# The first head's decay made in thirds between the small projections of a hybrid decoder block

## The chip, the cores and the metric

The kernel runs on one core of one Trainium2 chip. Its time is the device time of one execution in microseconds (us); what is compared is the median of three runs. The core has five engines that work beside each other, each through its own instruction queue and in that queue's order: PE (TensorE, matmuls), ACT (ScalarE, functions of single elements), DVE (VectorE, operations on one or two tensors and scans), POOL (GpSimd) and SP (SyncE, which here issues DMA transfers). An engine starts its next instruction when the semaphores that this instruction names have been raised by other engines or by transfers. Matmul results lie in PSUM, all else in SBUF.

## The reference, cut to what matters

A sequence of 1024 tokens with 16 meta tokens ahead of it (1040 columns, `T`) goes through one block: gated linear attention (GLA, 4 heads with 128 key channels and 256 value channels each) beside an mLSTM of 4 heads, then a gated MLP. All is float32. What the change touches is the decay of GLA's first head. `z` is the normalised input:

```python
log_a = jax.nn.log_sigmoid(g_lr @ w_gate + b_gate) / 16     # g_lr: 16 small channels of z @ w_in
bc    = cumsum(log_a)                                       # inside a chunk
score = sum_k q[t,k] * k[s,k] * exp(bc[t,k] - bc[s,k])      # s <= t
out   = (q * exp(bc)) @ S + score @ v
```

The kernel forms the decay as min(y, 0) - ln(1 + exp(-|y|)), which is log sigmoid of y, and sums it with a scan that starts anew at each chunk of 128 tokens.

## The kernel before, in words

**Input and precision.** The normalised input is transposed on PE into `xH` and `xL` (channels on the partitions, 8 tiles of 128 channels, tokens along the free axis): `xH` is the value rounded to PE's faster format, `xL` the rest. A weight is split in the same way, and a product is made of three matmuls (high by high, high by low, low by high).

**Projections.** `proj_cm` (L222) makes one projection in pieces of some 256 tokens. A piece is 24 matmuls (8 channel tiles by 3 products) into one of three PSUM banks (tag `pj`); ACT empties the bank with the bias into `kT` (L545) or `qT` (L554). The first head's key and query projections and the key projection of the second head, `k1`, are interleaved by `together` in `key_query_proj(0)` (L548 on): key, query, key 1, key, query, key 1, and so on. After six of these pieces the small projections stand.

**Small projections.** `small_proj` (L165) makes 40 rows at once: 16 low-rank gate channels and the input and forget gates of the mLSTM. It has three column groups `TH_ALL` of 348, 346 and 346 tokens, each of 16 matmuls into a `pj` bank (tile `plr`); ACT copies the lower half out and DVE adds bias and both halves into `lrs`.

**Decay.** `decay(0)` (L751) multiplies `lrs` by the gate weight: three groups of two matmuls into banks of the tag `s` (tiles `pre`). ACT takes the absolute value of each group, then exp of the whole row, then ln(1 + .) of the whole row, for which it loads another table of functions first; DVE takes the minimum of each group with 0, subtracts, and scans the whole row (`rmask` is 1, and 0 at each chunk's first token) into `bc`. `pack` (L187) copies `lrs` and the gate weight into `raw_s` and `wgp` for the heads that come later; POOL clears both first.

**Masks.** L509 to L531 make six 128x128 masks in the tile `mfs` on POOL, one memset and 22 `affine_select`; DVE copies the first to `flip` and the other five as bytes to `mu16` to `mu1`. `flip` is the matrix by which PE turns a tile of scores around (tile `sct`).

**Token sums.** `token_sums(0, nc.sync)` (L598) is work for a much later stage: eight sums and differences of 514 columns on POOL between the tiles `xa` and `xb`, stored by eight transfers that SP issues (L619). The two tiles have the tag `of` with two buffers. The next tile of that tag is `An` of the first head's scores: it takes the buffer of `xb`, the one after it that of `xa`.

**Scores of head 0.** `gla(0)` (L776) first makes the levels 1 to 64: at each level the product of the decayed key and the decayed query of half blocks of that size, with DVE, POOL and ACT taking parts (`level`, `pk` tiles). Level 1 begins with ACT's exp of the decay into `An` (L856). Then come the diagonal products (`kq`, L789 to L794), the turned tile (`sct`, L819) and PE's column sums of `kq` (L800, tile `sc`).

**What sets the order.** The program is written in generators that yield after each piece, and a scheduler moves instructions on each engine by priority: `hp(n)` lifts what is written inside it by n places, and `tc.issue_after(x)` holds it behind the instruction x. So evacuations and splits move forward, while PE's order stays near the written one. `main` (L1146) runs a projection's pieces and, 1.15 times to a piece, moves the generator at the head of `side`, here `gla(0)`, one step on.

Of the kernel before, what the change touches and what calls it, by code (L numbers as in the profile page):

```python
# [45 lines left out]
def hybrid_kernel(ctx, tc, x, meta, norm_mix, w_in, b_in, gla_w_gate, gla_b_gate, gla_norm,  # L46
# [118 lines left out]
    def small_proj():  # L165
# [5 lines left out]
        for t0, n in TH_ALL:  # L171
            pt = ps.tile([P, 512], F32, name=f"plr{t0}", tag="pj", bufs=3)
            for k in range(NK):
                first, both = (xL, 64), (xH, P)
                for j, (x, m) in enumerate((both, first) if k < NK - 1 else (first, both)):
                    nc.tensor.matmul(pt[:m, :n], lr2[:, k, :m], x[:, k, t0:t0 + n],
                                     start=(k == 0 and j == 0), stop=(k == NK - 1 and j == 1), skip_group_check=True)
            with hp(PRI_E):
                r = lrs[0:64, t0:t0 + n]
                nc.scalar.activation(r, pt[64:128, :n], AF.Copy)  # L180
                nc.vector.scalar_tensor_tensor(r, pt[0:64, :n], bsm[0:64], r, OP.add, OP.add)
            yield
        nc.gpsimd.dma_start(msc, lrs[32:40, :])

    decay_in = {}

    def pack():  # L187

        lrs, K = decay_in[0], NM + 1
        nc.gpsimd.memset(raw_s[0:96].bitcast(F32), 0.0)  # L190
# [316 lines left out]
    with tc.issue_after(last.ins):  # L507

        lmask = {}  # L509
        mfs = hd.tile([P, T], F32, name="mfs", tag="raw", bufs=1)  # L510
# [5 lines left out]
        nc.vector.tensor_copy(flip, mfs[:, :P])  # L516
# [3 lines left out]
        for i, b in enumerate((16, 8, 4, 2, 1)):  # L520
            mf = mfs[:, P * (i + 1):P * (i + 2)]
            nb = P // (2 * b)
            for odd in range(2):
                half = mf[:, 64 * odd:64 * odd + 64].rearrange("p (n w) -> p n w", w=b)
                for base, sg in (((P - 1) * odd, -1), (b - 1 - (P - 1) * odd, 1)):
                    nc.gpsimd.affine_select(out=half, in_=half, compare_op=OP.is_ge, fill=0.0, base=base,
                                            pattern=[[sg * 2 * b, nb], [0, b]],
                                            channel_multiplier=sg if odd else -sg)
            mu = hd.tile([P, P], U8, name=f"mu{b}")
            nc.vector.tensor_copy(mu, mf)  # L530
            lmask[b] = mu  # L531
# [16 lines left out]
    def key_query_proj(s):  # L548
        h = s % 4
        hh = heads.setdefault(s, {})  # L550
        if s < 4:
# [4 lines left out]
            if s == 0:  # L556
                k1 = key_proj(1)
                yield from islice(together(pk, pq, k1), 6)
                yield from small_proj()
                token_sums(0, nc.sync)  # L560
                pkq = together(pk, pq)
                yield from islice(pkq, 1)
                decay(0)
                pack()
                yield from pkq
                side.append(gla(0))
# [183 lines left out]

    def decay(s):  # L751
        la = wtile(f"la{s}")
        pre = []
        for t0, n in TH_ALL:
            pt = ps.tile([P, 512], F32, name=f"pre{s}_{t0}", tag="s", bufs=3)
            if s:
                w, x = wgp[0:65 + NM, P * (s - 1):P * s], raw_s[0:65 + NM]
            else:
                w, x = wg, decay_in[0][0:NM + 1]
# [1342 lines left out]
```

## Time and profile before

| | us |
|---|---|
| median of three runs | 1871.53 |
| lowest and highest run | 1869.77, 1873.11 |
| profiled execution | 1871.91 |
| its span in the trace | 1869.9 |

The granted clock of PE, averaged over the profiled span, is 0.997 of the full one. The rows that the prediction shows are of that execution. Names in them are cut to the program's names: `plr` and `pre` are the PSUM tiles of the small projections and of the decay, `pj` those of the key and query pieces, `la` and `bc` the two rows of the decay, `mfs`, `mu` and `flip` the masks, `xa` and `xb` the token sums, `pk` a level, `pv` the value projection. A row of the timeline gives the start from the beginning of the span, the time of the group, the engine, the tile or operation, and in square brackets the idle time of the engine ahead of it with what ended that.

### The profile page before, as it was taken

What the parts mean: (1) busy time and instruction counts of PE and PEld (TensorE: products, weight loads), DVE (VectorE), ACT (ScalarE), POOL (GpSimd) and SP (SyncE); (2) the same over time, 40 slices, a digit from 0 to 9 for tenths busy, and PEclk for the clock granted to TensorE, in tenths of its full rate; (3) what the DMA queues carried; (4) which work ended last, traced back from release to release, by engine and by line L of the source; (5) the groups of instructions that cost most, each with busy time, mean ns of one, the idle gap of its engine ahead of it and who ended that gap; (6) DMA issues with size and microseconds to landing.
All of it is one profiled execution on the core that took longest, in us unless ns stands there. A gap on an engine that the chain in (4) does not pass through costs nothing.

```text
span 1869.9 us, 32624 instructions
## 1 busy us (share of the span) xinstructions
PE 1847.2 (99%) x13286; PEld 1769.7 (95%) x13286; DVE 1227.2 (66%) x1817; ACT 868.8 (46%) x1394; POOL 429.8 (23%) x485
## 2 busy tenths in 40 slices
PE   8999999999999999999999999999999999999998
PEld 7899999999999999999999999999999999987886
DVE  7756757554563466655432547698887888787876
ACT  5465555545454433432422335543443443465664
POOL 6301101205442000123281510012222222200100
PEclk9999999999999999999999999999999999999999
DMA  5111022143324755665973643324333334288894
GB/s 164 56 37 60 23 61 60 35 116 122 96 77 125 195 139 144 159 181 158 335 240 113 221 152 125 124 86 131 118 103 113 108 102 130 86 321 317 284 385 166
DMA packets 221820, 269.63 MB, mean 144 GB/s; under 512 B 13986, under 2 KB 177101, under 8 KB 221671
## 3 DMA queue, kind: packets, MB, share of 16 engines
q1 hardware_dynamic: 200447, 196.20, 33.9%
q0 software_dynamic: 18624, 62.62, 10.1%
q10 hardware_dynamic: 2600, 8.74, 1.2%
q8 instruction: 104, 1.70, 0.4%
q14 instruction: 45, 0.37, 0.1%
HBM read 197.91 MB, written 69.60 MB: 143 GB/s over the span
## 4 chain that ended last, share of the span: by engine, by line
PE 88%; DVE 5%; DMA 3%; ACT 2%; issue 1%; SPq 0%; POOL 0%; POOLq 0%; ACTq 0%; DVEq 0%
PE pj L232 11%; PE pv L274 8%; PE Yu L1175 6%; PE Xu L1175 6%; PE Zu L1175 6%; PE bg L1414 5%; PE bm L1414 5%; PE Zg L1175 4%; PE Yg L1175 4%; PE Xg L1175 4%; PE po L1708 4%; PE Vu L1175 3%; PE pdX L1865 2%; PE pdZ L1865 2%; PE pdY L1865 2%; PE Vg L1175 2%
## 5 line engine op out<-in xcount | busy, mean ns | idle before, releaser
L638 POOL TENSOR_TENSOR ts<-ts 128x256 f32<-128x256 f32 x88 | 78.6, 899 | 49.4 <-DMA ts<-in_ffn_w_down_dram 47.4
L1621 POOL TENSOR_TENSOR SB<-SA,rg 128x512 f32<-128x512 f32 x20 | 32.7, 1637 | 239.7 <-issue 101.4
L274 PE MATMUL pv<-wH_gv,xH 128*128 128x256 f32 x256 | 75.0, 293 | 0.0
L274 PE MATMUL pv<-wH_mv,xH 128*128 128x256 f32 x256 | 74.8, 292 | 0.1
L880 POOL TENSOR_TENSOR pk<-pk,kT 128x256 f32<-128x256 f32 (+1 forms) x24 | 31.0, 1291 | 187.3 <-ACT pk L878 154.6
L274 PE MATMUL pv<-wH_gv,xL 128*128 128x256 f32 x256 | 72.6, 283 | 0.0
L1708 PE MATMUL po<-wH_wo,yH 128*128 128x256 f32 x256 | 72.5, 283 | 0.1
L274 PE MATMUL pv<-wL_gv,xH 128*128 128x256 f32 x256 | 72.5, 283 | 0.0
L274 PE MATMUL pv<-wL_mv,xH 128*128 128x256 f32 x256 | 71.9, 281 | 0.0
L1708 PE MATMUL po<-wL_wo,yH 128*128 128x256 f32 x256 | 71.7, 281 | 0.3 <-DVE wL_wo L147 0.3
L274 PE MATMUL pv<-wH_mv,xL 128*128 128x256 f32 x256 | 71.9, 281 | 0.0
L1708 PE MATMUL po<-wH_wo,yL 128*128 128x256 f32 x256 | 71.8, 281 | 0.0
L1656 DVE SCALAR_TENSOR_TENSOR cv<-u,fc,cv 128x1024 f32<-128x1024 f32 x44 | 65.1, 1482 | 0.4
L1603 POOL TENSOR_TENSOR A<-u2raw,A 128x512 fp32r<-128x512 f32 x20 | 42.5, 2124 | 86.2 <-ACT A L1602 86.2
L1414 PE MATMUL bg<-ogL,wH_bg 128*128 128x342 f32 x192 | 61.5, 320 | 0.0
L1414 PE MATMUL bg<-ogH,wH_bg 128*128 128x342 f32 x192 | 61.5, 320 | 0.0
L1414 PE MATMUL bm<-omH,wH_bm 128*128 128x342 f32 x192 | 61.4, 320 | 0.0
L1414 PE MATMUL bm<-omH,wL_bm 128*128 128x342 f32 x192 | 61.3, 319 | 0.0
L1414 PE MATMUL bg<-ogH,wL_bg 128*128 128x342 f32 x192 | 61.3, 319 | 0.0
L1414 PE MATMUL bm<-omL,wH_bm 128*128 128x342 f32 x192 | 61.2, 319 | 0.0
L278 DVE TENSOR_TENSOR v<-pv,bB 128x256 f32<-128x256 f32 x64 | 26.5, 417 | 40.3 <-PE pv L274 40.0
L1602 ACT ACTIVATE HA<-rg 128x1024 fp32r<-128x1024 f32 x16 | 17.0, 1061 | 73.0 <-PE Yu L1175 72.6
(814 smaller groups left out, 7511.5 us busy)
## 6 DMA issues: line engine op xcount, KB each, us to landing
gw<-in_w_in_dram SPq DMA_DIRECT2D x26, 512.0 KB, 5.4
ts<-in_ffn_w_down_dram POOLq DMA_DIRECT2D x44, 256.0 KB, 3.9
tdn<-ts POOLq DMA_DIRECT2D x44, 256.0 KB, 3.1
rg<-in_ffn_w_up_dram SPq DMA_DIRECT2D x22, 512.0 KB, 3.9
ru<-in_ffn_w_up_dram SPq DMA_DIRECT2D x22, 512.0 KB, 3.9
adr<-s SPq DMA_DIRECT2D x40, 256.0 KB, 3.0
rd<-in_ffn_w_down_dram SPq DMA_DIRECT2D x20, 512.0 KB, 11.4
do<-tdn SPq DMA_DIRECT2D x18, 512.0 KB, 5.5
```

Of the source, the lines that this page charges most:

```text
L232: nc.tensor.matmul(pt[:, :n], a[:, k, :], b[:, k, base + t0:base + t0 + n], start=(i == 0), stop=(i == 3 * NK - 1))
L274: nc.tensor.matmul(pt[:, :DV], a[:, k, t0:t0 + P], b[:, k % 4, :], start=(i == 0), stop=(i == 3 * NK - 1))
L278: nc.vector.tensor_tensor(vt[:n, c, :DV], pt[:n, :DV], bB[:n, :], OP.add)
L638: nc.gpsimd.tensor_tensor(t[:, o], t[:, a], t[:, b], OP.subtract)
L880: eng.tensor_tensor(e, e, k, OP.mult)
L1175: nc.tensor.matmul(out[:, :n], x[:, k, :], y[:, k, :], start=start and k == 0 and j == 0, stop=stop and k == 3 and j == 2, skip_group_chec ...
L1414: nc.tensor.matmul(pt[:, i, :n], a[:, k, :], b[k][:, base + t0:base + t0 + n], start=(k == 0 and j == 0), stop=(k == NK - 1 and j == 2))
L1603: eng.tensor_tensor(l, src, h.bitcast(F32), OP.subtract)
L1621: late.tensor_tensor(sb[:, 0:4], sa[:, 0:4], rg[:, 0:4], OP.subtract)
L1656: nc.vector.scalar_tensor_tensor(y, u[:, j:SEQ + j], fc[:, j, jj:jj + 1], y, OP.mult, OP.add)
L1708: nc.tensor.matmul(pt[:, :DV], a, b[:, k % 4, :], start=(k == 0 and i == 0), stop=(k == NK - 1 and i == len(terms) - 1))
L1865: nc.tensor.matmul(banks[r, j, b][:, c], p, q[:, c], start=first and k == 0, stop=last and k == 2, skip_group_check=True)
```

## The change

The first head's decay gets a function of its own, `first_decay`. It is a generator with one step for each third of the columns: a `pre` product, ACT's Abs and Exp and DVE's minimum of that third. It is advanced once after the second and once after the third small projection, so that the first two thirds are made there; the last third follows after one key piece, where the whole decay stood. The logarithm, the subtraction and the scan are then made in two halves (columns 0 to 528 and 528 to 1040; at 528 a chunk begins, so the second scan starts at 0).

The small projections come after five pieces of the interleaved projections in place of six; the sixth (second piece of `k1`) follows the first head's last key and query pieces. `raw_s` is cleared by a function of its own, `clear`, which is called ahead of the small projections. The tile `mfs` takes a buffer of the tag `r`, which an input tile had, in place of `raw`. The copies of the masks on DVE (`keep_masks`) are held behind the last sum of the small projections (`joined`), the token sums behind the clearing and the last `affine_select` (`masked`). `decay`, for the other heads, is the same but for the branch that head 0 had.

```diff
--- before.py
+++ after.py
@@ -178,16 +178,18 @@
             with hp(PRI_E):
                 r = lrs[0:64, t0:t0 + n]
                 nc.scalar.activation(r, pt[64:128, :n], AF.Copy)
-                nc.vector.scalar_tensor_tensor(r, pt[0:64, :n], bsm[0:64], r, OP.add, OP.add)
+                joined[:] = [nc.vector.scalar_tensor_tensor(r, pt[0:64, :n], bsm[0:64], r, OP.add, OP.add).ins]
             yield
         nc.gpsimd.dma_start(msc, lrs[32:40, :])
 
-    decay_in = {}
+    decay_in, joined = {}, []
+
+    def clear():
+        return nc.gpsimd.memset(raw_s[0:96].bitcast(F32), 0.0)
 
     def pack():
 
         lrs, K = decay_in[0], NM + 1
-        nc.gpsimd.memset(raw_s[0:96].bitcast(F32), 0.0)
         nc.gpsimd.memset(wgp.bitcast(F32), 0.0)
         src = lrs[64:64 + K, :3 * P]
         for p0 in (0, 32):
@@ -507,13 +509,12 @@
     with tc.issue_after(last.ins):
 
         lmask = {}
-        mfs = hd.tile([P, T], F32, name="mfs", tag="raw", bufs=1)
+        mfs = hd.tile([P, T], F32, name="mfs", tag="r", bufs=2)
         nc.gpsimd.memset(mfs[:, :P * 6], 1.0)
         for sg in (1, -1):
             nc.gpsimd.affine_select(out=mfs[:, :P], in_=mfs[:, :P], compare_op=OP.is_ge, fill=0.0, base=-sg * (P - 1),
                                     pattern=[[sg, P]], channel_multiplier=sg)
         flip = hd.tile([P, P], F32, name="flip")
-        nc.vector.tensor_copy(flip, mfs[:, :P])
         mu = hd.tile([P, P], U8, name="mu0")
         nc.vector.tensor_copy(mu, ident)
         lmask[0] = mu
@@ -523,12 +524,15 @@
             for odd in range(2):
                 half = mf[:, 64 * odd:64 * odd + 64].rearrange("p (n w) -> p n w", w=b)
                 for base, sg in (((P - 1) * odd, -1), (b - 1 - (P - 1) * odd, 1)):
-                    nc.gpsimd.affine_select(out=half, in_=half, compare_op=OP.is_ge, fill=0.0, base=base,
+                    masked = nc.gpsimd.affine_select(out=half, in_=half, compare_op=OP.is_ge, fill=0.0, base=base,
                                             pattern=[[sg * 2 * b, nb], [0, b]],
                                             channel_multiplier=sg if odd else -sg)
-            mu = hd.tile([P, P], U8, name=f"mu{b}")
-            nc.vector.tensor_copy(mu, mf)
-            lmask[b] = mu
+            lmask[b] = hd.tile([P, P], U8, name=f"mu{b}")
+
+    def keep_masks():
+        nc.vector.tensor_copy(flip, mfs[:, :P])
+        for i, b in enumerate((16, 8, 4, 2, 1)):
+            nc.vector.tensor_copy(lmask[b], mfs[:, P * (i + 1):P * (i + 2)])
 
 
     osc = {g: dram.tile([NK, P, NP], F32, name=f"osc{g}") for g in "gm"}
@@ -555,14 +559,25 @@
                 qT[:, t0:t0 + n], p, AF.Identity, bias=cc(C_GQ + h), scale=QS))
             if s == 0:
                 k1 = key_proj(1)
-                yield from islice(together(pk, pq, k1), 6)
-                yield from small_proj()
-                token_sums(0, nc.sync)
+                yield from islice(together(pk, pq, k1), 5)
+                parts = first_decay()
+                with tc.issue_after(last.ins):
+                    cleared = clear()
+                for i, _ in enumerate(small_proj()):
+                    if i:
+                        next(parts)
+                    yield
+                with tc.issue_after(joined[0]):
+                    keep_masks()
+                with tc.issue_after(cleared.ins), tc.issue_after(masked.ins):
+                    token_sums(0, nc.sync)
                 pkq = together(pk, pq)
                 yield from islice(pkq, 1)
-                decay(0)
+                for _ in parts:
+                    pass
                 pack()
                 yield from pkq
+                yield from islice(k1, 1)
                 side.append(gla(0))
                 yield from k1
             else:
@@ -748,15 +763,33 @@
     def state(name):
         return hd.tile([P, DV + 1], F32, name=name, tag="S", bufs=4)
 
+    def first_decay():
+
+        la = wtile("la0")
+        bc = hd.tile([P, T], F32, name="bc0", tag="bc")
+        heads.setdefault(0, {})["decay"] = la, bc
+        for t0, n in TH_ALL:
+            pt = ps.tile([P, 512], F32, name=f"pre0_{t0}", tag="s", bufs=3)
+            nc.tensor.matmul(pt[:, :n], wg, decay_in[0][0:NM + 1][:, t0:t0 + n], start=True, stop=True)
+            with hp(PRI_E):
+                l = la[:, t0:t0 + n]
+                nc.scalar.activation(l, pt[:, :n], AF.Abs)
+                exped = nc.scalar.activation(l, l, AF.Exp, scale=-1.0)
+                lowest = nc.vector.tensor_scalar(bc[:, t0:t0 + n], pt[:, :n], 0.0, None, OP.min)
+            yield
+        half = NM + SEQ // 2
+        with hp(PRI_E), tc.issue_after(exped.ins), tc.issue_after(lowest.ins):
+            for c in (slice(0, half), slice(half, T)):
+                nc.scalar.activation(la[:, c], la[:, c], AF.Ln, bias=one1)
+                nc.vector.tensor_tensor(la[:, c], bc[:, c], la[:, c], OP.subtract)
+                nc.vector.tensor_tensor_scan(bc[:, c], rmask[:, c], la[:, c], 0.0, OP.mult, OP.add)
+
     def decay(s):
         la = wtile(f"la{s}")
         pre = []
         for t0, n in TH_ALL:
             pt = ps.tile([P, 512], F32, name=f"pre{s}_{t0}", tag="s", bufs=3)
-            if s:
-                w, x = wgp[0:65 + NM, P * (s - 1):P * s], raw_s[0:65 + NM]
-            else:
-                w, x = wg, decay_in[0][0:NM + 1]
+            w, x = wgp[0:65 + NM, P * (s - 1):P * s], raw_s[0:65 + NM]
             nc.tensor.matmul(pt[:, :n], w, x[:, t0:t0 + n], start=True, stop=True)
             pre.append((pt, t0, n))
         if s == 3:
```

The order on three engines, around the copies and around An. First POOL, from the masks to the end of the token sums (`xa`, `xb`); before:

```order
L604 TENSOR_TENSOR xa_682<-xH,xL 128x514
L412 TENSOR_TENSOR xr_365<-xv_363,mhalf 128x1
L511 MEMSET mfs 128x768
L513 AFFINE_SELECT mfs<-mfs 128x128
L526 AFFINE_SELECT mfs<-mfs 128x64 x2
L513 AFFINE_SELECT mfs<-mfs 128x128
L526 AFFINE_SELECT mfs<-mfs 128x64 x18
L604 TENSOR_TENSOR xa_682<-xH,xL 128x514
L607 TENSOR_TENSOR xb_683<-xa_682 128x514
L604 TENSOR_TENSOR xb_683<-xH,xL 128x514
L604 TENSOR_TENSOR xa_682<-xH,xL 128x514
L607 TENSOR_TENSOR xa_682<-xb_683,xa_682 128x514
```

and with the change:

```order
L513 MEMSET mfs 128x768
L188 MEMSET raw_s 96x1040
L515 AFFINE_SELECT mfs<-mfs 128x128
L527 AFFINE_SELECT mfs<-mfs 128x64 x2
L515 AFFINE_SELECT mfs<-mfs 128x128
L527 AFFINE_SELECT mfs<-mfs 128x64 x18
L619 TENSOR_TENSOR xa_669<-xH,xL 128x514 x2
L622 TENSOR_TENSOR xb_670<-xa_669 128x514
L619 TENSOR_TENSOR xb_670<-xH,xL 128x514
L619 TENSOR_TENSOR xa_669<-xH,xL 128x514
L622 TENSOR_TENSOR xa_669<-xb_670,xa_669 128x514
L622 TENSOR_TENSOR xb_670<-xb_670 128x514
```

The first sum of `xa` has moved behind the masks, and the clearing of `raw_s`, which stood before the last two sums, into the masks.

Second DVE, from the masks' copies to the decay; before:

```order
L516 COPY flip<-mfs 128x128
L530 CAST mu_402<-mfs 128x128
...
L530 CAST mu_426<-mfs 128x128
L181 SCALAR_TENSOR_TENSOR lrs<-plr_624,bsm,lrs 64x348
L181 SCALAR_TENSOR_TENSOR lrs<-plr_643,bsm,lrs 64x346
L181 SCALAR_TENSOR_TENSOR lrs<-plr_662,bsm,lrs 64x346
L198 TENSOR_TENSOR raw_s<-lrs,raw_s 17x1040
L769 TENSOR_SCALAR bc_733<-pre_0_727 128x348
```

and with the change:

```order
L181 SCALAR_TENSOR_TENSOR lrs<-plr_638,bsm,lrs 64x346
L533 COPY flip<-mfs 128x128
L778 TENSOR_SCALAR bc_632<-pre_348_657 128x346
L535 CAST mu_401<-mfs 128x128
...
L535 CAST mu_421<-mfs 128x128
L200 TENSOR_TENSOR raw_s<-lrs,raw_s 17x1040
L778 TENSOR_SCALAR bc_632<-pre_694_713 128x346
L784 TENSOR_TENSOR la_631<-bc_632,la_631 128x528
L784 TENSOR_TENSOR la_631<-bc_632,la_631 128x512
L785 SCALAR_TENSOR_TENSOR bc_632<-rmask,la_631 128x528
```

The copy to `flip` and the five casts have moved from ahead of the sums of the small projections to between the second and the last third of the decay; the row L785 is the first half of the scan.

Third ACT, from the last third of the decay to An; before:

```order
L768 ACTIVATE la_726<-pre_694_731 128x346
L770 ACTIVATE la_726<-la_726 128x1040
L771 ACT_TABLE_LOAD
L771 ACTIVATE la_726<-la_726,one_79 128x1040
L554 ACTIVATE qT_441<-pj_514_752,col 128x256
L856 ACT_TABLE_LOAD
L856 ACTIVATE An_856<-la_726 128x512
```

and with the change:

```order
L776 ACTIVATE la_631<-pre_694_713 128x346
L777 ACTIVATE la_631<-la_631 128x346
L783 ACT_TABLE_LOAD
L783 ACTIVATE la_631<-la_631,one_79 128x528
L783 ACTIVATE la_631<-la_631,one_79 128x512
L889 ACT_TABLE_LOAD
L889 ACTIVATE An_861<-la_631 128x512
L558 ACTIVATE qT_435<-pj_514_731,col 128x256
```

The evacuation of the query piece from 514 on, which frees a `pj` bank, stood ahead of the second table load and now stands behind An.

## The prediction, made before the changed kernel was run

> **What bounds the kernel now.** I read the busy table first.
>
> ```profile
> span 1869.9 us, 32624 instructions
> PE 1847.2 (99%) x13286; PEld 1769.7 (95%) x13286; DVE 1227.2 (66%) x1817; ACT 868.8 (46%) x1394; POOL 429.8 (23%) x485
> ```
>
> The matrix engine (PE) is busy for 99% of the span and the change takes no matmul away, so all it can win is PE's idle time, or PE time at a lowered clock. The profiled execution took 1871.91 us: 2.0 more than its span, 0.4 more than the median of the runs, 1871.53. Next the windows (start and end, length, busy time of PE, weight loads, DVE, ACT and POOL, then the granted clock, DMA share, GB/s), cut in steps of 3.41 us, on whose edges the clock changes:
>
> ```profile
> 30.47:33.88 3.41, 1.98 (x18) 1.96 (x18) 3.00 (x7) 3.07 (x7) 0.62 (x2) 1.00 0.29 75
> ...
> 88.50:91.91 3.41, 1.67 (x4) 0.53 (x4) 2.60 (x6) 0.63 (x1) 1.30 (x1) 1.00 0.00 0
> 91.91:95.33 3.42, 2.74 (x9) 2.14 (x10) 3.34 (x5) 2.17 (x3) 0.00 (x0) 0.50 0.00 0
> 95.33:98.74 3.41, 3.41 (x17) 3.31 (x16) 1.73 (x3) 1.46 (x5) 0.00 (x0) 0.50 0.00 0
> ```
>
> One place behind the change stands out: PE is half idle from 88.5 us on, and then runs at half clock from 91.91 to 98.74. The timeline of PE (start, time taken, instruction, and in brackets how long PE was idle and for whom) shows the scores of head 0 there, waiting for the vector engine (DVE):
>
> ```profile
> 87.36 0.28 PE L274 MATMUL pv<-wH_gv,xL 128*128 128x256 f32 x1
> 89.68 1.12 PE L819 MATMUL sct<-A,flip 128*128 128x512 f32 x2 [2.04 <-DVE A L846]
> 91.14 0.50 PE L800 MATMUL sc<-kq,ones 128*128 128x512 f32 x1 [0.34 <-ACT kq L793]
> 91.87 0.79 PE L800 MATMUL sc<-kq,ones 128*128 128x512 f32 x1 [0.22 <-DVE kq L794]
> 93.34 0.80 PE L800 MATMUL sc<-kq,ones 128*128 128x512 f32 x1 [0.68 <-ACT kq L793]
> ```
>
> Now the chain that ended last, for the price of PE's pieces at full clock:
>
> ```profile
> 40.51 7.57 PE plr L176 x48
> 48.08 2.80 PE pj L232 x24
> 50.88 1.94 PE pre L760 x6
> 52.83 8.72 PE pj L232 x72
> ...
> 100.26 0.89 PE sc L829 x8
> 101.15 2.84 PE pv L274 x24
> ```
>
> The product that starts at 87.36 gives way after 2.84/24 = 0.12, at 87.48. From there to 98.7 PE does the two sct matmuls (1.1), four column sums of 512 columns (0.9 by the pv step, which has 256), eight score matmuls (0.9) and some twelve value products (1.4): 4.3 us of work in 11.1 (to 98.6). So **6.8 us are lost here**, half in waits and half in clock. That is the most that this change can win.
>
> DVE is late because it has no slack: from 65.5 on it works at the levels of head 0, 23.5 of 24.1 us.
>
> ```profile
> 65.50:89.60 24.10, 22.08 (x185) 21.58 (x183) 23.50 (x42) 8.92 (x11) 9.99 (x6) 1.00 0.23 64
> ```
>
> These levels begin when the decay is scanned, on DVE, and its logarithm made, on the scalar engine (ACT):
>
> ```profile
> 57.56 1.24 DVE L772 TENSOR_TENSOR la<-bc,la 128x1040 f32<-128x1040 f32 x1 [2.91 <-ACT la L771]
> 58.84 2.32 DVE L773 TENSOR_TENSOR_SCAN bc<-rmask,la 128x1040 f32<-128x1040 f32 x1
> ```
>
> ```profile
> 56.37 1.17 ACT L771 ACTIVATE la<-la,one 128x1040 f32<-128x1040 f32 x1
> 57.44 0.45 ACT L554 ACTIVATE qT<-pj,col 128x256 f32<-128x256 f32 x1
> 58.87 1.28 ACT L856 ACT_TABLE_LOAD   x1 [0.98 <-issue]
> 60.17 0.67 ACT L856 ACTIVATE An<-la 128x512 f32<-128x512 f32 x1
> 61.20 0.22 ACT L921 ACTIVATE dl<-bc 128x8 f32<-128x8 f32 x1 [0.36 <-DVE bc L773]
> ```
>
> ACT's dl at 61.20 starts as the scan ends (61.16), and the weights and levels stand behind it. Call d the shift of that moment. The second kq, which PE takes at 93.34, moves by d too.
>
> **The change, part by part.**
>
> *The projections one piece ahead.* A key piece of 24 matmuls (2.80) now stands behind the small projections, which start about 3.1 earlier, at 37.4 (two small transposes are 0.3 of it). PE's work stays the same. The last `pre` would end at 52.83 - 3.1 = 49.7, and the three pieces behind it (8.72 in the row, 2.81 each) at 58.2.
>
> *The decay by parts.* The first two thirds of Abs and Exp run on ACT between the small projections; there PE feeds ACT, which has room. Behind the last third stand on ACT 0.4 (Abs), 0.4 (Exp), 1.28 (table), and the logarithm in halves of 0.6: 50.0 to 53.3. On DVE two subtractions (0.64 each) end at 54.0 and two half scans (1.17 each) at 56.3, against 61.16. The three further ACT and two further DVE instructions are inside these times. With nothing else in the way d would be -4.8.
>
> *The copies and POOL.* This is where the gain can be lost. The masks' tile moves to a buffer that an x tile leaves just as early, so the masks start as before, but now `raw_s` is cleared ahead of them, and all eight token sums come behind them; one of the eight used to run earlier, in a gap.
>
> ```profile
> 34.01 0.74 POOL L511 MEMSET mfs<- 128x768 f32 x1
> ...
> 42.87 1.30 POOL L604 TENSOR_TENSOR xa<-xH,xL 128x514 f32<-128x514 f32 x1
> ...
> 49.24 0.96 POOL L190 MEMSET raw_s<- 96x1040 f32 x1
> 50.16 1.28 POOL L607 TENSOR_TENSOR xb<-xb 128x514 f32<-128x514 f32 x1
> 51.52 2.20 POOL L607 TENSOR_TENSOR xa<-xa,xb 128x514 f32<-128x514 f32 x1
> ```
>
> 34.75 + 0.95 + 8.1 of selects = 43.7; five sums took 6.37, so 1.27 each, and eight end at 53.9 if nothing stops them. Meanwhile DVE wants to copy the masks:
>
> ```profile
> 42.93 1.33 DVE L530 CAST mu<-mfs 128x128 uint8<-128x128 f32 x1 [1.77 <-POOL mfs L526]
> ...
> 51.34 1.23 DVE L198 TENSOR_TENSOR raw_s<-lrs,raw_s 17x1040 fp32r<-17x1040 f32 x1 [2.16 <-ACT raw_s L197]
> ```
>
> The cast that met a sum took 1.33, as long as the sum, and the sum that met DVE's `raw_s` took 2.20 instead of 1.28: one engine stops while the other runs. Much later sums and DVE's short `wt` steps met as well:
>
> ```profile
> 548.28 2.76 DVE L1038 SCALAR_TENSOR_TENSOR wt<-MB,tcol,big 128x128 f32<-128x128 f32 x2
> ```
>
> Two steps of 128 columns took 2.76 in all, one sum's length for each: they take turns. Of the Trainium skill, the page "SBUF — State Buffer", section "Who interferes with whom", states this as a lock: DVE with two SBUF inputs, or copying in a two-port mode, and POOL exclude each other for a whole instruction, in order of issue. That speaks against this change, and by it alone the half scans would be held up as well, about 1.3 us for each turn lost; the rows above show casts and subtractions held, no scan.
>
> I take turns as the likeliest. The flip copy and five casts are asked for from 47 us on (behind the third small projection), in the middle of the sums. Each cast waits for one sum: they end at about 54.2, `raw_s` (1.1) at 55.3, the last minimum (0.5) at 55.8, the two subtractions at 57.0, the scans at 59.3. In exchange the sums are stopped little and end at 54. Then ACT: table 57.0 to 58.3, An to 59.0, and qT, which now stands behind An on ACT, to 59.4. So d = 59.4 - 61.2 = **-1.8**.
>
> *PE's new wait.* Key 1's next piece, at 58.2, needs the bank that this qT empties: it waits until 59.5, **1.3**. Later, unhindered, PE would reach the second kq at 87.48 + 1.1 + 0.45 = 89.05, now at 90.35; kq is there at 93.3 - 1.8 = 91.5: **1.15** more. The clock stays full, I assume: a window with PE busy 1.98 of 3.41 (30.47) was followed by full clock, one with 1.67 (88.50) by half. The Trainium skill's page "TensorE: Matmul & The Clock Gate", section "HAM oscillation", asks only that no idle gap exceed about 3.4 us. By it these two gaps cost no clock either, but the 2.04 before sct did, so here the row decides.
>
> *Sum.* Lost after: 1.3 + 1.15 = 2.45; lost before: 6.8. 1871.91 - 4.35 = 1867.6 in the profiled execution's terms, less the 0.4: **1867.2**. Behind the scores nothing is added.
>
> Bounds. If POOL and DVE never met, the last store that An's buffer waits for (the seventh sum, 52.6, and the store) would set An:
>
> ```profile
> tsc<-xb SPq DMA_DIRECT2D x2, 128.0 KB, 1.9
> ```
>
> Two issues 0.4 apart and 1.9 of landing: 55.0; table, An and qT to 57.4, no new wait of PE, d = -3.8, kq at 89.5: 0.45 lost, 1865.2. If DVE kept the port from the casts through the scans, see the first rival.
>
> **Rivals.**
>
> *An waits for the store (the slower side).* An's buffer was xb: its stores must land first. If DVE's casts and `raw_s` run in one go, sums six and seven start after 50.5 us; if the subtractions and scans (to 56.5) then shut POOL out as well, the seventh sum ends at 57.8, its store lands near 60.2, and ACT stands still, with qT behind the wait: table to 61.5, An to 62.2, qT to 62.7. PE idles from 58.2 to 62.7, 4.5; a window almost without work is followed by half clock until a full one has passed (as 91.91 to 98.74), some 5.4 us of work at half rate, 2.7. With another sum's delay (1.3) it is 8.5 lost against 6.8: 1873.2. It decides when the store lands later than 60. For it, a POOL product of 1.2 that DVE's row of subtractions and products held up:
>
> ```profile
> 76.74 3.11 POOL L880 TENSOR_TENSOR pk<-pk,kT 128x256 f32<-128x256 f32 x1 [3.98 <-ACT pk L878]
> ```
>
> Against it: the turns above.
>
> *No conflict:* 1865.2, as above. For it: no row shows a scan held up, and the sums' own needs in the row at 42.87 were met in full.
>
> *The gain is used up on the way* (the change does not do what it says): casts, `raw_s` and scans are pushed so far that the scan ends near 61 again, d = 0: 4.25 lost at kq in any case, and half clock for one window (1.7) more: 1870.7. For it: all of these stand in one row on DVE, before the subtractions.
>
> **How the numbers follow.** Forecast 0.43 (1866 to 1868.6), store 0.22, no conflict 0.18, used up 0.17. The range goes from 1864.7 (no conflict, less the spread) to 1873.2, the slower rival; the forecast's own is 1866.0 to 1868.6. About 0.2% (3.7 us) is what a measurement here tells from no change: faster means below 1867.8, slower above 1875.3. Faster: no conflict 0.18 and two thirds of the forecast, 0.29, together 0.47. Slower: 0.11, the tail of the store rival with a second half-clock stretch. The rest, 0.42, is the same.
>
> **What would show it.** Right: An starts near 58.3 and the scans end near 59.3; casts of about 1.3 each between the sums; a wait of PE of 1 to 2 us on ACT's qT near 58; at sct no wait for A, one of about 1 for kq; no half clock. Wrong: An after 61 with ACT waiting for a DMA (first rival); casts of 0.3 and scans done by 57 (no conflict); sct still waiting for DVE's A by over a microsecond (used up). A loss anywhere behind 105 us would be none of these.

## The result, and the profile of the changed kernel

The changed kernel took 1866.42 us (median of 7 runs, 1863.82 to 1868.84) against 1871.53 before (also 7 runs): a ratio of 0.997, with a 95% interval from 0.9958 to 0.9981. It is faster by some 5 us, 0.3%; the prediction was 1867.2. The profiled execution took 1867.16, 4.75 less than that of before. Its busy table shows the same work in a shorter span:

```profile
span 1865.1 us, 32629 instructions
PE 1846.0 (99%) x13286; PEld 1768.5 (95%) x13286; DVE 1227.9 (66%) x1819; ACT 869.8 (47%) x1397; POOL 427.5 (23%) x485
```

The place that the prediction had marked is closed. PE's timeline at head 0's scores, in the changed kernel, answers to the four waits shown of before (2.04, 0.34, 0.22 and 0.68):

```profile
86.55 1.02 PE L852 MATMUL sct<-A,flip 128*128 128x512 f32 x2
87.01 1.03 PE L833 MATMUL sc<-kq,ones 128*128 128x512 f32 x2
88.26 0.50 PE L833 MATMUL sc<-kq,ones 128*128 128x512 f32 x1 [0.21 <-ACT kq L826]
```

One wait of 0.21 is left, and the windows (PE busy first, granted clock third from the end) show full clock where half was granted from 91.91 to 98.74:

```profile
88.50:91.91 3.41, 3.41 (x27) 3.17 (x27) 3.02 (x6) 2.35 (x6) 0.00 (x0) 1.00 0.00 0
91.91:95.33 3.42, 3.42 (x31) 3.42 (x30) 2.16 (x3) 1.83 (x3) 0.00 (x0) 1.00 0.00 0
```

What lies ahead of it, first on DVE from the copy to `flip` on:

```profile
45.83 1.29 DVE L533 COPY flip<-mfs 128x128 f32<-128x128 f32 x1
47.05 0.50 DVE L778 TENSOR_SCALAR bc<-pre 128x346 f32<-128x346 f32 x1
47.48 3.65 DVE L535 CAST mu<-mfs 128x128 uint8<-128x128 f32 x5
51.16 2.22 DVE L200 TENSOR_TENSOR raw_s<-lrs,raw_s 17x1040 fp32r<-17x1040 f32 x1
53.41 0.52 DVE L778 TENSOR_SCALAR bc<-pre 128x346 f32<-128x346 f32 x1
53.84 1.30 DVE L784 TENSOR_TENSOR la<-bc,la 128x528 f32<-128x528 f32 x2
55.06 2.37 DVE L785 TENSOR_TENSOR_SCAN bc<-rmask,la 128x528 f32<-128x528 f32 x2
```

Then two of POOL's token sums beside them, and ACT at the same place:

```profile
49.61 1.30 POOL L622 TENSOR_TENSOR xb<-xb 128x514 f32<-128x514 f32 x1
50.99 1.29 POOL L622 TENSOR_TENSOR xa<-xa,xb 128x514 f32<-128x514 f32 x1
```

```profile
55.21 1.28 ACT L889 ACT_TABLE_LOAD   x1 [2.13 <-DVE la L784]
56.51 0.68 ACT L889 ACTIVATE An<-la 128x512 f32<-128x512 f32 x1
57.09 0.46 ACT L558 ACTIVATE qT<-pj,col 128x256 f32<-128x256 f32 x1
```

The copies and `raw_s` are slowed (3.65 for five casts, 2.22 for a product that took 1.23 before), the sums are not, and the scan ends at 57.43 instead of 61.16. The table load before An waits for DVE's subtraction, not for a store. Nothing waits for `qT`, but it is close: `qT` is done at 57.55, and the next piece starts in its bank at 57.92.

Behind the scores PE was 7.3 us ahead of the execution before, and 7.1 still near 1640; the span shrank by 4.8. The difference was lost in one place there, where the up projection hands over to the down projection. ACT there waits for a transfer, PE for ACT, and then PE runs at half clock for one window; the rows of ACT, of PE and of the windows (cut on the edges of that fall) in the changed kernel, and PE's row of before:

```profile
1639.94 1.06 ACT L1877 ACTIVATE dw<-dy 128x1024 fp32r<-128x1024 f32 x1 [2.88 <-DMA dy<-adr]
```

```profile
1641.05 0.51 PE L1898 MATMUL pdV<-dy,dw 128*128 128x512 f32 x1 [1.74 <-ACT dw L1877]
```

```profile
1639.32:1642.73 3.41, 1.16 (x4) 0.68 (x5) 1.70 (x3) 2.51 (x3) 0.00 (x0) 1.00 1.04 402
1642.73:1646.14 3.41, 3.41 (x10) 2.63 (x9) 3.41 (x4) 3.41 (x4) 0.00 (x0) 0.50 1.04 416
```

```profile
1647.07 0.50 PE L1865 MATMUL pdV<-dy,dw 128*128 128x512 f32 x1 [0.68 <-ACT dw L1844]
```

From the start of the up projection's last matmul to that of the 23rd of the down projection, which is called the handover below, PE took 6.99 us before and 9.60 here. Of these 2.6 some 1.7 are the 3.41 at half clock (an estimate: half of that window), the rest is the longer wait. No step of the prediction knew of this loss; whether it belongs to the change is one of the questions below.

### The profile page after: what moved, and what is told of

Same layout as the page of the kernel before. It is cut to its first block, busy times and chain, and to the rows that moved or that the text cites. A ratio compares the mean times of both kernels' runs of the same rounds, so it can differ in the third digit from the quotient of the medians.

```text
span 1865.1 us, 32629 instructions
## 1 busy us (share of the span) xinstructions
PE 1846.0 (99%) x13286; PEld 1768.5 (95%) x13286; DVE 1227.9 (66%) x1819; ACT 869.8 (47%) x1397; POOL 427.5 (23%) x485
## 5 line engine op out<-in xcount | busy, mean ns | idle before, releaser
L1447 PE MATMUL bm<-omL,wH_bm 128*128 128x342 f32 x192 | 61.2, 319 | 0.0
```

The source lines that it names most:

```text
L1447: nc.tensor.matmul(pt[:, i, :n], a[:, k, :], b[k][:, base + t0:base + t0 + n], start=(k == 0 and j == 0), stop=(k == NK - 1 and j == 2))
```

## The experiments

Each kernel is the changed one with the edit shown. Medians are of 6 to 12 runs; the kernel before took 1871.7 to 1871.8 beside E1 to E8, 1871.05 beside E9 and E10. To compare the executions free of what happens at the start and at the end, three numbers are read from each trace. The **start** is the matmul from which PE has the same 360 matmuls left up to the transposes of `kh` (tile `k0t`), behind head 0's scores: 52.75 before, 52.24 with the change. The **lag** is the end of the scan less this start. The **stretch** is PE's time from the start to `k0t`:

```profile
103.83 0.27 PE L932 MATMUL k0t<-ident,kh 128*16 128x128 f32 x1
```

```profile
96.52 0.27 PE L965 MATMUL k0t<-ident,kh 128*16 128x128 f32 x1
```

So it took 51.1 before (103.83 - 52.75) and 44.3 with the change (96.52 - 52.24); the least in any run is 44.2.

| kernel | scan ends | lag | stretch above 44.2 | handover | median |
|---|---|---|---|---|---|
| before | 61.2 | 8.4 | 6.9 | 7.0 | 1871.5 |
| changed | 57.4 | 5.2 | 0.1 | 9.6 | 1866.4 |
| E1 whole logarithm and scan | 57.5 | 5.4 | 0.4 | 5.9 | 1865.2 |
| E2 piece put back | 58.8 | 6.8 | 2.9 | 5.9 | 1868.6 |
| E3 copies ahead | 60.1 | 3.9 | 0.0 | 7.6 | 1870.1 |
| E4 sums as memsets | 55.9 | 3.9 | 0.0 | 8.9 | 1865.8 |
| E5 sums later | 59.4 | 7.1 | 9.9 | 7.6 | 1875.5 |
| E6 minimum six times | 61.9 | 8.0 | 3.9 | 6.6 | 1868.6 |
| E7 first sum ahead | 57.1 | 4.2 | 0.0 | 7.2 | 1866.8 |
| E8 no thirds | 58.9 | 6.9 | 1.8 | 6.2 | 1866.4 |
| E9 changed, again | 57.7 | 5.2 | 0.0 | 7.8 | 1866.0 |
| E10 before, again | 63.1 | 8.5 | 6.8 | 7.2 | 1870.4 |

### E1: the halves undone

```diff
-            for c in (slice(0, half), slice(half, T)):
+            for c in (slice(0, T),):
```

> The changed kernel with logarithm, subtraction and scan of the first head made whole again, everything else as changed. Theory (what counts is when the scan ends, and ahead of it DVE is busy with the product for raw_s and the last minimum until 53.9 us anyway): the whole logarithm ends near 52.9, the subtraction runs 53.9 to 55.1, the scan ends near 57.4 as in the changed kernel; time within 0.5 us of the changed kernel's 1866.4. Rival (the halves carry the gain, since subtraction and logarithm overlap): the scan ends 1.2 later, at 58.6, PE waits about 1 us more at head 0's scores, near 1867.6.

Measured: 1865.16, ratio 0.9969 (0.9958 to 0.998). DVE's rows of this run:

```profile
53.86 1.24 DVE L784 TENSOR_TENSOR la<-bc,la 128x1040 f32<-128x1040 f32 x1
55.13 2.32 DVE L785 TENSOR_TENSOR_SCAN bc<-rmask,la 128x1040 f32<-128x1040 f32 x1
```

The scan ends where it does with halves (57.45). DVE is busy with `raw_s` and the last minimum until 53.9, and by then the whole logarithm is done. The median lies 1.3 below the changed kernel's, outside the 0.5 expected, but the two intervals against the kernel before nearly coincide. The halves bring 0.3 of the stretch at most, and nothing that the medians show.

### E2: the key piece put back

```diff
-                yield from islice(together(pk, pq, k1), 5)
+                yield from islice(together(pk, pq, k1), 6)
...
-                yield from islice(k1, 1)
```

> The changed kernel with six pieces ahead of the small projections again, so that the decay starts one key piece (2.8 us) later. Theory (part of the 2.8 is given back because the copies then meet fewer token sums): scan ends near 58.8 against 57.4, PE waits 1 to 1.5 us for kq at the scores, no half clock: 1867.0 to 1868. Rival (the piece ahead is nearly the whole gain): scan ends at 60.2, PE waits 2.5 to 3 us and the clock falls to half again: 1869.5 or more.

Measured: 1868.55, ratio 0.9984 (0.9975 to 0.9993). The scan ends at 58.80, as the theory said, but PE's waits at the scores come to 2.2, more than it said:

```profile
87.22 1.12 PE L851 MATMUL sct<-A,flip 128*128 128x512 f32 x2 [0.63 <-DVE A L878]
88.69 0.50 PE L832 MATMUL sc<-kq,ones 128*128 128x512 f32 x1 [0.35 <-ACT kq L825]
89.42 0.50 PE L832 MATMUL sc<-kq,ones 128*128 128x512 f32 x1 [0.23 <-DVE kq L826]
90.89 0.50 PE L832 MATMUL sc<-kq,ones 128*128 128x512 f32 x1 [0.98 <-ACT kq L825]
```

All four waits of before are there. The first is much smaller (0.63 for 2.04), the middle two are the same, the last is larger (0.98 for 0.68), and the clock stays full. The piece ahead is worth some 2.8 of the stretch, although it moves the scan by only 1.4: with the piece back, the copies meet fewer sums and `raw_s` takes 1.23.

### E3: the copies of the masks ahead of the sums again

```diff
         flip = hd.tile([P, P], F32, name="flip")
+        nc.vector.tensor_copy(flip, mfs[:, :P])
...
             lmask[b] = hd.tile([P, P], U8, name=f"mu{b}")
+            nc.vector.tensor_copy(lmask[b], mf)
...
-                with tc.issue_after(joined[0]):
-                    keep_masks()
```

> The changed kernel with the copies of the masks ahead of the sums of the small projections again. Theory: DVE stands before the casts until the last select of POOL (41.9 us), so the first sum of the small projections, at 39.34 in the changed kernel, is made at 42.1 and PE waits about 1.4 us for it ahead of the first product of the decay; behind that DVE meets fewer token sums and the scan still ends near 57. Time 1.2 to 1.5 us above the changed kernel: 1867.6 to 1868. Rival (PE has other work there): no wait of PE above 0.3 at 41 us, the scan ends earlier than 57.4, time within 0.4 of the changed kernel.

Measured: 1870.05, ratio 0.9991 (0.9983 to 1.0), 3.6 above the changed kernel. DVE's last cast waits for POOL's last select, then meets a sum; PE waits for what stands behind it, and the window after runs at half clock:

```profile
41.87 1.29 DVE L532 CAST mu<-mfs 128x128 uint8<-128x128 f32 x1 [1.75 <-POOL mfs L528]
43.08 1.05 DVE L181 SCALAR_TENSOR_TENSOR lrs<-plr,bsm,lrs 64x348 f32<-64x348 f32 x2
```

```profile
43.70 1.03 PE L771 MATMUL pre<-lrs,wg 17*128 17x348 f32 x2 [2.55 <-DVE lrs L181]
```

```profile
44.10:47.50 3.40, 3.40 (x12) 2.52 (x11) 0.55 (x2) 0.95 (x2) 3.32 (x4) 0.52 0.22 77
```

The place of the wait was as expected, its price not: 2.55 and the clock in place of 1.4; the start moves from 52.2 to 56.2. Behind it nothing is lost, for the lag is only 3.9. With the small projections one piece earlier, the copies have to stand behind their sums: without that edit most of the gain is gone. (What it would do alone, without the piece ahead, no run shows.)

### E4: POOL without reading

```diff
-            nc.gpsimd.tensor_tensor(dst, x, y, OP.subtract)
+            nc.gpsimd.memset(dst, 0.5) if k == 0 else nc.gpsimd.tensor_tensor(dst, x, y, OP.subtract)
```

and the same for the additions.

> The changed kernel with the eight token sums of the first channel tile on POOL replaced by memsets of the same tiles (these sums are left out of the computation), so that POOL reads nothing there. Theory (POOL's sums hold DVE up, and after the change the scores have no loss left to win): casts take about 0.2 each, raw_s 1.1 instead of 2.22, the scan ends near 56.2, 1.2 earlier, and the time stays within 0.5 us of the changed kernel's 1866.4. Rival (the decay still sets PE's end): the time falls by about 1.0 to 1865.4. If memsets hold DVE up like sums, casts of 1.3 remain.

Measured: 1865.82, ratio 0.9968 (0.9957 to 0.998). DVE's rows:

```profile
46.32 0.76 DVE L535 CAST mu<-mfs 128x128 uint8<-128x128 f32 x5
47.37 1.23 DVE L200 TENSOR_TENSOR raw_s<-lrs,raw_s 17x1040 fp32r<-17x1040 f32 x1 [0.30 <-ACT raw_s L199]
...
53.49 2.37 DVE L786 TENSOR_TENSOR_SCAN bc<-rmask,la 128x528 f32<-128x528 f32 x2
```

Five casts take 0.76 instead of 3.65, `raw_s` 1.23 instead of 2.22; the scan ends at 55.86, 1.6 earlier, held by the logarithm alone. Of the 1.6 some 0.2 are this execution's earlier start; the lag is 1.3 shorter. The median is 0.6 lower, between the two expectations and within the scatter of the runs. The trace decides: the stretch was 0.1 above its floor and is now on it. (The memsets were done before the casts began, so this run shows what the casts cost without POOL, not what memsets do to them; E5 shows that.) So the meetings of DVE and POOL cost the decay 1.3 us and the kernel 0.1 at most.

### E5: the store rival made on purpose

```diff
         first, second = T0, T0 + 512
+        if k == 0:
+            for _ in range(12):
+                nc.gpsimd.memset(a[1], 0.5)
```

> The changed kernel with twelve memsets of 0.5 us on POOL put among the first token sums, so that the last six sums and the stores that An's buffer waits for come some 6 us later; nothing is left out. This is the first rival of the prediction made on purpose: sums beside the raw_s product, the subtractions and the scans. By the prediction's price: the store lands behind 60, An starts at 61.5 or later, PE stands 3 to 5 us for the query piece's bank at 58 and loses another 1 to 3 at half clock: the time rises by 5 to 8 us over the changed kernel's 1866.4, to 1871.5 or more. The rival reading (PE has enough other work and An is not waited for): An late, but PE waits less than 1 us and the time stays within 1 us. Apart from that it shows whether sums hold up subtractions (0.7 becomes 1.3 or more) and scans (1.2 becomes 2 or more), which no trace so far shows.

Measured: 1875.45, ratio 1.0019 (1.001 to 1.0028), 9 above the changed kernel and one more than the 5 to 8 expected. ACT, PE, and DVE beside POOL:

```profile
62.90 1.28 ACT L892 ACT_TABLE_LOAD   x1 [9.78 <-DMA tsc<-xb]
```

```profile
65.27 0.58 PE L234 MATMUL pj<-xH,wH_gk 128*128 128x256 f32 x1 [7.15 <-ACT qT L558]
```

```profile
52.54 2.42 DVE L787 TENSOR_TENSOR la<-bc,la 128x528 f32<-128x528 f32 x2 [2.06 <-ACT la L786]
54.87 4.51 DVE L788 TENSOR_TENSOR_SCAN bc<-rmask,la 128x528 f32<-128x528 f32 x2
```

```profile
56.06 2.25 POOL L619 TENSOR_TENSOR xa<-xH,xL 128x514 f32<-128x514 f32 x1
```

The slower rival of the prediction is a real mechanism: An waits for the store of `xb`, `qT` stands behind An, and PE behind `qT`'s bank for 7.15 us, with the clock at half when it goes on (0.50 from 65.00 to 68.41). Scans and subtractions are held by sums, and sums by them (two half scans in 4.51 instead of 2.37, a sum in 2.25 instead of 1.29). The changed kernel escapes because its seventh sum ends at 50.91, before the subtractions begin at 53.84. How much room that leaves can be estimated from the rows. In E5 the table load started 2.45 after the end of the sum (60.45); 2.45 after 50.91 is 53.36, and the changed kernel's load started at 55.21, so that An has 1.9 to spare. `qT` has another 0.4. If nothing else moves, some 2.2 us more of POOL work ahead of that sum would make PE wait for the bank; the memsets of E5 came to 6.9.

### E6: aimed at the forecast's own state

```diff
-                lowest = nc.vector.tensor_scalar(bc[:, t0:t0 + n], pt[:, :n], 0.0, None, OP.min)
+                for _ in range(6 if t0 > 348 else 1):
+                    lowest = nc.vector.tensor_scalar(bc[:, t0:t0 + n], pt[:, :n], 0.0, None, OP.min)
```

> The changed kernel with the last minimum made six times over on DVE (the same values), so that the scan ends some 2.2 us later, near 59.6: the state that the prediction had forecast (59.3). By the prediction's price PE then waits about 1.3 for the query piece's bank and 1.15 at the scores: behind the scores PE stands some 2.2 later than in the changed kernel, near 1868.6. The theory now, from the run with the piece put back (scan end 58.8, four waits of 2.2 in all at the scores): 1.3 to 1.8 at the bank and 2 to 3 at the scores, 3.5 to 4.5 later, near 1870.

Measured: 1868.62, ratio 0.9986 (0.9977 to 0.9995). The median is the prediction's price, 2.2 above the changed kernel, yet by another way. The order on ACT changed with the edit, and `qT` came ahead of An again:

```profile
54.62 0.46 ACT L558 ACTIVATE qT<-pj,col 128x256 f32<-128x256 f32 x1
59.65 1.28 ACT L890 ACT_TABLE_LOAD   x1 [4.57 <-DVE la L785]
```

So PE never waited for the bank of `qT`. It waited 0.42 for that of a key piece (at 62.98) and lost the rest of the 3.9 at the scores, where two waits of 0.23 and 0.97 were followed by a window of half clock:

```profile
89.42:92.83 3.41, 2.17 (x7) 0.88 (x6) 2.88 (x5) 1.82 (x4) 0.00 (x0) 1.00 0.00 0
92.83:96.24 3.41, 3.41 (x16) 3.31 (x16) 1.81 (x3) 1.35 (x3) 0.00 (x0) 0.50 0.00 0
```

This execution had started 1.6 later from its first loads on, and its lag of 8.0 is above the 6.8 that the forecast amounts to. It neither bears out nor refutes the wait of 1.3 at the bank.

### E7: the first token sum ahead again

```diff
-                with tc.issue_after(cleared.ins), tc.issue_after(masked.ins):
-                    token_sums(0, nc.sync)
+                token_sums(0, nc.sync)
```

> The changed kernel with the token sums no longer held behind the masks and the clearing, so that the first of them runs at 29 to 31 us again as in the kernel before. Theory: PE's gaps for the normalised x tiles at 30 to 34 us return (about 1.3 us, the start of the small projections moves from 35.9 to about 37), and the sums end 1.3 earlier; the scan ends within 0.5 of 57.4, PE arrives later at the scores by about 0.7 and waits no more there: time within 1 us above the changed kernel. Rival (holding the sums back matters only for the copies): no gap at 30 us, time the same or 0.5 lower because casts meet fewer sums.

Measured: 1866.84, ratio 0.9975 (0.9966 to 0.9984). PE's gap for an x tile is back, as it was in the kernel before, while the sums end earlier and leave `raw_s` alone:

```profile
31.27 0.63 PE L425 MATMUL xtp<-ident,xt 128*128 128x128 f32 x4 [1.43 <-DVE xt L417]
```

```profile
51.78 1.23 DVE L200 TENSOR_TENSOR raw_s<-lrs,raw_s 17x1040 fp32r<-17x1040 f32 x1
```

In the changed kernel this gap is 0.42. Of that 1.0 some 0.6 is left at the start (52.86 against 52.24), and the lag of 4.2 is worth nothing. By the medians the two are not told apart.

### E8: the thirds in one row

```diff
-                for i, _ in enumerate(small_proj()):
-                    if i:
-                        next(parts)
-                    yield
+                yield from small_proj()
```

> The changed kernel with all three thirds of the first head's decay made where the last one stands, behind the key piece; pieces, copies, sums and halves as changed. Theory: three Abs and three Exp then stand on ACT ahead of the table load and three minima on DVE behind the raw_s product; subtractions start near 54.9 to 55.3 instead of 53.8, the scan ends near 58.7, and PE loses some 2 us more at the scores (as with the piece put back): 1868 to 1869. Rival (the thirds change nothing, since DVE is held until 53.4 in any case): scan end within 0.4 of 57.4, time within 0.5 of the changed kernel.

Measured: 1866.43, ratio 0.9973 (0.9964 to 0.9982). The scan ends at 58.86, as the theory said:

```profile
46.38 5.18 DVE L535 CAST mu<-mfs 128x128 uint8<-128x128 f32 x5
53.99 1.37 DVE L775 TENSOR_SCALAR bc<-pre 128x348 f32<-128x348 f32 x3
56.50 2.36 DVE L782 TENSOR_TENSOR_SCAN bc<-rmask,la 128x528 f32<-128x528 f32 x2
```

The stretch is 1.7 longer than the changed kernel's. The start is 0.3 earlier, because PE does the six small products in one place. That leaves 1.4 in the trace, and none in the median. By the trace the thirds are worth something, by the time it isn't shown.

Two things in this run bear on the prediction. Its lag, 6.9, is that of E2 and of the forecast, yet PE waits only twice at the scores, not for A, and the clock stays full:

```profile
88.17 0.50 PE L830 MATMUL sc<-kq,ones 128*128 128x512 f32 x1 [0.23 <-DVE kq L824]
89.64 0.51 PE L830 MATMUL sc<-kq,ones 128*128 128x512 f32 x1 [0.97 <-ACT kq L823]
```

And its casts took 5.18, not 3.65: three in a row waited for one sum each.

### E9 and E10: both kernels again, unaltered

> The changed kernel once more, unaltered. Theory: all that the change does lies before 92 us and repeats within 0.3 (scan end 57.4, no wait of PE above 0.3 at the scores); the 2.5 us that the first profile of the changed kernel lost near 1640, where ACT waits for a transfer, belong to that execution: the time from the last Zu product to the tenth row of the down projection lies anywhere between 5.9 and 9.6, as in the runs so far. Rival (arriving earlier makes PE wait there): it is 9 or more again.

> The kernel before once more, unaltered. Theory: the loss of 6 to 7 us at head 0's scores with a stretch of half clock is there again (scan end 8.4 behind PE's piece, within 0.3), and the stretch near 1645 differs by chance. Rival: the half clock was a matter of that one execution, and the loss is 4 us or less now.

Measured: 1866.02, ratio 0.9978 (0.9968 to 0.9988), and 1870.42, ratio 1.0 (0.9991 to 1.0009). PE's rows at the scores, first of the changed kernel, then of the one before:

```profile
88.50 0.50 PE L833 MATMUL sc<-kq,ones 128*128 128x512 f32 x1 [0.18 <-ACT kq L826]
```

```profile
91.62 1.13 PE L819 MATMUL sct<-A,flip 128*128 128x512 f32 x2 [2.02 <-DVE A L846]
93.08 0.50 PE L800 MATMUL sc<-kq,ones 128*128 128x512 f32 x1 [0.34 <-ACT kq L793]
93.81 0.79 PE L800 MATMUL sc<-kq,ones 128*128 128x512 f32 x1 [0.23 <-DVE kq L794]
95.28 0.80 PE L800 MATMUL sc<-kq,ones 128*128 128x512 f32 x1 [0.68 <-ACT kq L793]
```

Everything up to the scores repeats to 0.1: the lags 5.2 and 8.5, the stretch 44.2 and 51.0, the four waits one by one. The start of the program does not: the second execution of the kernel before began its pieces at 54.64 instead of 52.75. Nor does the handover, 7.8 instead of 9.6 with the change. There SP issues the transfer that ACT waits for 5.80 us ahead of the same matmul in all twelve executions, whenever that matmul comes; only the landing differs, and the handover takes 5.9 to 9.6 with the same instructions. E1 and E2 came there 7.3 and 4.7 us earlier than the kernel before and passed in 5.9. Arriving early does not lengthen it by itself.

This leaves one thing open in part. At the handover PE is 7.1 us ahead of the first profile of the kernel before, and the medians differ by 5.1 (5.0 in E9). Half clock at the handover stands in two of the twelve profiles, the changed kernel's and E4's, and these two take longest there (9.6 and 8.9, the others 5.9 to 7.8). Runs without a profile have a mean granted clock. At 0.999 there is no room for such a window beside the half clock behind the last matmuls, at 0.998 there is. Of the changed kernel's seven runs the three at 0.999 have a median of 1864.19, the four at 0.998 of 1866.85; in E9 it is 1865.32 (four) and 1868.11 (five). On the other side, 16 of the 75 runs of the kernel before beside the experiments also have 0.999, too high a mean for the 6.8 us at half clock that both its profiles show at the scores. Both pull the medians closer together than the lead. Where a run without a profile lost its clock is not known, so I can't say that this is all of it.

## Why the prediction was right, and where it wasn't

**The place and its size.** The loss of 6.8 us at head 0's scores was named as the most that could be won, and 6.8 of the stretch's 6.9 were won (51.1 to 44.3). PE's half clock went with its waits, as assumed.

**The start.** The small projections were to start some 3 us earlier and the pieces behind the last `pre` at 49.7; it was 49.33. A gain that the prediction put at nothing is the sum that moved behind the masks: it had stood ahead of POOL's part in normalising an x tile, and PE's gap for that tile shrank from 1.43 to 0.42 (E7 brings it back). The three separate products of the decay cost some of it again.

**The turns of DVE and POOL.** This is the step that failed: d was -3.7 and not -1.8. The prediction had "each cast waits for one sum", with casts until 54.2, `raw_s` until 55.3 and the scan until 59.3. The casts ended at 51.1, and the scan at 57.4. The copies were asked for 1.2 earlier than forecast (45.83 against 47), and `flip` and the casts together took 5.3 (with a minimum of 0.5 among them) and not 7.2, since not every cast waited for a sum of its own. Twice a cast of 0.21 slipped in right behind one that had waited, each time where POOL left 0.08 between two sums (49.53 to 49.61, 50.91 to 50.99). In E8 three casts in a row waited one sum each, where the sums followed without such a gap. So turns are real, but how many a row of short copies takes depends on the order of the sums. `raw_s` then met the last sum and took 2.22, which the forecast did not have. The meetings cost the scan 1.3 (E4), not 3. The prediction also had subtractions among what its rows show held; its rows show casts and `wt` steps, and a held subtraction came only with E5 (1.79 for one of 0.69). Of the Trainium skill, the page "SBUF — State Buffer", section "Who interferes with whom", has the lock go to the instruction that was issued first, and held for all of it; the rows of the changed kernel and E5 agree, and E5 adds what no row had shown before, a scan held: 2.34 for one of 1.2.

**The wait for the bank.** The prediction's 1.3 rested on `qT` at 59.4 and did not occur, since `qT` was done at 57.55. It was the term that hung on the failed step. E5 shows that the wait itself is real (7.15), E6 that the scheduler can take it away. The size of 1.3 was not tested.

**The waits at the scores.** The forecast's scan end of 59.3 and start of 52.5 make a lag of 6.8. Two runs have it, and they differ. E8 lost 1.8, with no wait for A and 0.97 for the second kq, much as the prediction said (1.15). E2 lost 2.9: there four products in a row wait, the first for A. So the 1.15 was of the right kind for one order of the pieces and too little for the other; why A is late in E2 and not in E8, at the same lag, stays open.

**The sum.** 6.8 at the scores and 0.5 at the start make 7.3; the profiled execution had 7.1 of it left at the handover and lost 2.6 there. So 4.75 against the predicted 4.35 is near by two errors of opposite sign: too little gained, and a loss late in the program that the prediction had ruled out of its terms. That is luck. Without the 2.6 the profiled execution would have taken some 1864.5, below the forecast's own 1866.0 to 1868.6.

**The rivals.** "No conflict" was wrong as a mechanism (3.65 and 2.22 are conflicts) but near in its d: -3.8, there set by the store, where -3.7 was measured, set by the scan. "Used up" did not happen. The store rival was held off by some 2 us of POOL time (estimated at E5).

## What to carry to other kernels

- What an earlier chain is worth depends on its lag behind the engine that sets the end, and there is a knee. Here all lag up to 5.4 costs 0.4 at most, and the 3 us from there to 8.4 cost 6.5. Below the knee, further work on the chain (E4) or on its parts (E1) buys next to nothing. Above it the lag alone does not give the price: 6.8 and 6.9 cost 2.9 and 1.8, 8.0 cost 3.9, 8.4 cost 6.9, partly by whether the clock falls. (The 9.9 of E5 are the bank's.)
- Before copies and products are put beside sums on POOL, count which of them meet, and in what order they are issued: a short copy can slip through between two sums (two of five in the changed kernel, one of five in E8), a long one is held for a whole sum.
- A buffer that is freed by a store, and a bank that is emptied behind its user, are a chain across ACT and PE that is invisible until it is late. Here it was some 2 us away by the estimate, and E5 ran into it.

## What the runs showed of the hardware

- Memsets on POOL slow DVE's copies but not its product. In E5, beside memsets of 0.53, five casts took 1.77 in all (0.76 alone in E4), and `raw_s` 1.23, as in E4 and E7 with nothing beside it; beside a sum it took 2.22. The Trainium skill's page "SBUF — State Buffer", section "SBUF: two separate sides", makes the same difference: an instruction of DVE with two inputs from SBUF contends only with POOL instructions that read there. Minima that read PSUM took 0.50 to 0.52 beside sums and without.
- The clock fell to half behind windows of 3.41 us, cut in steps from the edges of each profile's falls, in which PE was busy for 0.86 (E3, with a single wait of 2.55), 1.16 (the changed kernel's handover), 1.51 and 1.67 (before, at the scores) and 1.80 us (E4's handover). It stayed full behind 1.90 (E9's handover), 1.98 (before, from 30.47) and 2.43 and 2.20 (E2, with four waits of 2.2 in all). E6 does not fit: 2.17 was followed by half clock. So the busy share of one window does not settle it alone. Of the Trainium skill, the page "TensorE: Matmul & The Clock Gate", section "HAM oscillation", asks only that no gap exceed about 3.4 us; by that rule E3's gap would have cost nothing, and the run shows that it did.
- Transfers scatter between executions. ACT, waiting for a transfer, starts on the second input tile between 7.52 (E4) and 9.52 us (E10), and the transfer at the handover, issued at the same distance from the same matmul, lets ACT start up to 2.2 us apart. The two executions of the kernel before reach the same matmul at 52.75 and 54.64; 0.9 of that is the second input tile. Whether such scatter, with the clock that it costs, makes up all of the 5 us by which the runs of the changed kernel differ is not shown.
